# Two dense layers on one core: attention cut into more steps, put in another order among the projections, and queued behind them

## The chip, the cores and the metric

The kernel runs on one core of a Trainium2 chip. The metric is the time of one execution on the device in microseconds (us), as the median of several runs. TensorE (PE in the profile) multiplies matrices, VectorE (DVE) and ScalarE (ACT) work elementwise and read TensorE's results from PSUM, GpSimd (POOL) works elementwise in SBUF, and SyncE (SP) issues the transfers of the weights.

## The reference, cut to what matters

A first block (a token mixer and a mixture of experts) produces `x`, 256 tokens of 1024 channels. The second block puts 16 meta tokens ahead of them (272 rows) and runs two dense layers. The change touches the first half of each layer:

```python
for l in range(2):
    u = rmsnorm(h, norm_mix[l])
    proj = u @ w_in[l]                      # 13 pieces: qa ka va qi ki wi qb kb vb qc kc vc gc
    # A: 8 heads; 8 index heads score every key, the best 64 keys of a query are kept, softmax over them
    # B: 4 heads of two softmaxes each, w = p0 - lam * p1, then rmsnorm
    # C: 4 heads of retention (scores times a fixed decay), rotary q and k, rmsnorm, times silu(gc)
    h = h + concatenate([a_out, b_out, c_out]) @ w_out[l]
    u = rmsnorm(h, norm_ff[l])
    h = h + square(relu(u @ w_ff1[l])) @ w_ff2[l]
return rmsnorm(h, final_norm)[:, 16:]
```

## The kernel before

**Projections.** Activations stand with channels on the 128 partitions and the 272 tokens along the free axis. Every float32 operand is split into a high and a low part of a narrower type (`split_hl`, L148: the high part is a cast on ACT, the low part a subtraction on DVE), and a product is three matmuls per 128 input channels, high by high, high by low, low by high (`mm3`, L154, the matmul at L164). One projection (`prod`, L1609) makes 128 output channels: 8 blocks of input channels, so 24 matmuls of 272 columns. In layer 1, query-like pieces leave the meta tokens out and have 256 columns. `wload` brings 256 output channels of weights per transfer (1 MB) into a ring of four on SP's queue, which serves two projections; `parts` (L175) splits them into a ring of two.

**The mixing half of a layer** is a set of Python generators, `streams`: each `next()` traces one step. `b B u q k w c C y g` are projections (`cols`), each step one `prod`, its reading from PSUM, and for `u w y` three transposes (`to_keys`, L1661), for `c C` a rotary product (`rotated`, L1855), for `g` a silu. `I` is `indexer`: eight steps with score products (L1700) and then sixteen top-k steps that are DVE work alone (L1720, L1721). `A` is `attention`, four pairs of heads; `D` is `differential`, two pairs; `R` is `retention`, two pairs. `p` and `P` (`project`) multiply the first and the second half of the concatenated heads with `w_out`, eight steps of 12 matmuls each; before the first `p` the rest of `A`, before the first `P` the rest of `D` and `R` is traced. The projections of the indexer's inputs stand ahead of all of this and do not change.

**A step of attention before.** `attention`: scores of two query tiles, in layer 0 of the 16 meta rows too (L1788, L1797), bias plus selection on POOL (L1792), softmax (`softmax`, L1737: row minimum with the bias on DVE at L1742, exponential and row sum on ACT at L1743, reciprocal L1744, multiply L1746), end of the step; then the transposes of both heads on TensorE (`transposed`, L1755, matmuls at L1760 to L1764, copies back on ACT at L1766 and L1767), the products with the values (`pv_pair`, L1770, the matmul at L1776) and the split of the result, end of the step. `differential`: per head and query tile the scores (L1839) and two softmaxes that are joined at L1846, then two ends of a step in a row; after the tiles of a head its transposes; after both heads the value products and `head_norm` (L1806), which belong to the next step. `retention`: scores (L1881) times decay (L1883), value products and `head_norm` in one step.

**What sets the order.** `ORDER` (L1525) is a string per layer, written out by hand: one letter, one step. The order of tracing is a priority, not the issue order: the framework's scheduler fills each engine's queue from the instructions that its own reckoning has ready, the earliest traced first. So a step of attention can land in the middle of the 24 matmuls of a projection. On the chip each engine works through its queue in order. PSUM: three banks (`qm`) for results of projections and value products, two pairs (`qp`) for scores, transposes and norms, one bank (`qt`).

Of the kernel before, what the change touches and what calls it, by code (L numbers as in the profile page):

```python
# [9 lines left out]
F32 = mybir.dt.float32  # L10
F32R = mybir.dt.float32r
I32 = mybir.dt.int32
AF = mybir.ActivationFunctionType
# [140 lines left out]
def mm3(nc, out, terms, start, stop):  # L154

    n = 0
    for low in range(2):
        for wh, wl, xh, xl, fixed in terms:  # L160
            for w, x in (((wl, xh),) if low else ((wh, xh), (wh, xl))):
                l, r = (w, x) if fixed else (x, w)
                n += 1
                nc.tensor.matmul(out, l, r, start=start and n == 1, stop=stop and n == 3 * len(terms))  # L164


def load_w(k, src):
# [1280 lines left out]
def phase2_setup(k, one, tmp, psum):  # L1448
# [62 lines left out]
    for l in range(2):  # L1511
# [10 lines left out]

ORDER = ["IbIbIBIIIIIDIuDIIIqIDqIIDqkqDIIIDkIkIDwIDDDuBIIDDDDIIwDIwDIDIIIDIADDIgDgDIDDDDDAAcIkwAcDAADCCDDDAADyADyAApRpDDDRRppRpPpppPPPPPPPI",  # L1525
         "IIbIbBIIIIIDIuBIIuIDIDIDIIqqIkIDDIkIDDDIkkDIDDDIqqIDDIIIIIIAcIIwIDIDADDIDwcADDDDDDDwgDwADCACAAAyAyDADDDgARpDDDppRRpPppppPPRPPPDPP"]
T2 = 272
KT = ((0, 16), (16, 128), (144, 128))

# [1 line left out]
def phase2(k, q, A, B, out):  # L1531
# [5 lines left out]
    col = lambda name, i: vecT[:, r0[name] + i:r0[name] + i + 1]  # L1537
# [16 lines left out]
    def lgps(cols=512):  # L1554
        return pair(cols)[:, 0, :]
# [47 lines left out]
    def wload(src):  # L1603
# [2 lines left out]
        nc.sync.dma_start(w, src.rearrange("(k p) c -> p k c", p=128))  # L1606
        return w

    def prod(w, uh, ul, c0, o=None, first=True, last=True):  # L1609

        wh, wl = parts(k, w)
        m = w.shape[-1]
        if o is None:
            o = mmps(T2 - c0)
        mm3(nc, o[:m], [(wh[:, kk, :], wl[:, kk, :], uh[:, kk, c0:], ul[:, kk, c0:], True) for kk in range(w.shape[1])],
            first, last)
        return o[:m]

    nc.vector.tensor_copy(hT[:, :, 0:16], q["meT"])
# [16 lines left out]
    def layer(l, norm, end):  # L1636

        last = l == 1
# [98 lines left out]
        def softmax(pd, b, scaled, into=None):  # L1737

            m, n = pd.shape
            p = soft(m, n, "pd") if into is None else into  # L1740
            st = wk.tile([128, 3], F32, name=k.nm("st3"), tag="st3", bufs=4)[:m]
            nc.vector.tensor_tensor_reduce(p, pd, b, -1.0, 3.0e38, ALU.add, ALU.min, st[:, 0:1])  # L1742
            nc.scalar.activation(p, p, AF.Exp, bias=st[:, 0:1], scale=-1.0, accum_out=st[:, 1:2])  # L1743
            nc.vector.reciprocal(st[:, 2:3], st[:, 1:2])  # L1744
            if scaled:
                nc.vector.tensor_scalar_mul(p, p, st[:, 2:3])  # L1746
            return p, st[:, 2:3]

        def keys(t, j, n=128):
# [29 lines left out]
        def attention(hp):  # L1779

            rows = [slice(64 * i, 64 * i + 64) for i in range(2)]
            br = [bias_rows(2 * hp + i) for i in range(2)]
            p01, pm = ([], []), [None, None]
            for qt in range(2):
                ke = 144 + 128 * qt
                pd = pair(ke)
                for i in range(2):
                    nc.tensor.matmul(pd[:, i], qa[hp][rows[i], 16 + 128 * qt:144 + 128 * qt], ka[hp][rows[i], :ke],  # L1788
                                     start=True, stop=True)
                for i in range(2):  # L1790
                    bs = soft(128, ke)
                    nc.gpsimd.tensor_add(bs, bias_tile(br[i], qt), sels[qt])  # L1792
                    p01[i].append(softmax(pd[:, i], bs, True, bs)[0])
            if not last:
                pd = pair(16)
                for i in range(2):
                    nc.tensor.matmul(pd[:16, i], qa[hp][rows[i], 0:16], ka[hp][rows[i], 0:16], start=True, stop=True)  # L1797
                for i in range(2):
                    pm[i] = softmax(pd[:16, i], bmeta[:, 2 * hp + i, :], True, soft(16, 16))[0]
            yield 1  # L1800
            ts = [transposed(p01[i], pm[i], "pT") for i in range(2)]
            o = pv_pair(va[hp], ts)
            split_hl(k, cat_h[:, hp, c0:], cat_l[:, hp, c0:], o[:, c0:])
            yield 1

        def head_norm(o, gcol, extra, mul, j):  # L1806

            sq = wk.tile([128, T2], F32, name=k.nm("sq"), tag="sq", bufs=2)
            nc.scalar.activation(sq[:, c0:], o[:, c0:], AF.Square)
            pss = lgps(T2)  # L1810
            nc.tensor.matmul(pss[:, c0:], blk64, sq[:, c0:], start=True, stop=True)
            v = wk.tile([128, T2], F32, name=k.nm("nv"), tag="nv", bufs=1)
            nc.scalar.activation(v[:, c0:], pss[:, c0:], AF.Identity, scale=1.0 / 64, bias=k.eps)
            rs = wk.tile([128, T2], F32, name=k.nm("hrs"), tag="hrs", bufs=1)
            rsqrt_small(k, wk, rs[:, c0:], v[:, c0:], T2 - c0, tag="rq", full=T2)
            of = wk.tile([128, T2], F32, name=k.nm("of"), tag="of", bufs=2)
            nc.vector.scalar_tensor_tensor(of[:, c0:], o[:, c0:], gcol, rs[:, c0:], op0=ALU.mult, op1=ALU.mult)
            if mul is not None:
                nc.vector.tensor_mul(of[:, c0:], of[:, c0:], mul[:, c0:])
            if extra is not None:  # L1820
                nc.vector.tensor_scalar_mul(of[:, c0:], of[:, c0:], extra)
            split_hl(k, cat_h[:, j, c0:], cat_l[:, j, c0:], of[:, c0:])

        def differential(hp):
            ts = []
            for i in range(2):
                h = 2 * hp + i
                p01 = []
                br = bias_rows(8 + h)
                for qt in list(range(2)) + ([] if last else [2]):  # L1830
                    ke = 16 if qt == 2 else 144 + 128 * qt
                    qs = slice(0, 16) if qt == 2 else slice(16 + 128 * qt, 144 + 128 * qt)
                    nq = 16 if qt == 2 else 128
                    b = bmeta[:, 8 + h, :] if qt == 2 else bias_tile(br, qt)
                    pc, rc = [], []
                    pd = pair(ke)[:nq]
                    for c in range(2):
                        rows = slice(64 * i + 32 * c, 64 * i + 32 * c + 32)
                        nc.tensor.matmul(pd[:, c], qb[hp][rows, qs], kb[hp][rows, :ke], start=True, stop=True)  # L1839
                    for c in range(2):  # L1840
                        p, rr = softmax(pd[:, c], b, False)
                        pc.append(p)
                        rc.append(rr)
                    nc.vector.tensor_scalar(pc[1], pc[1], rc[1], nlam[:nq, l:l + 1], op0=ALU.mult, op1=ALU.mult)
                    w2 = wk.tile([128, T2], F32, name=k.nm("w2"), tag="w2", bufs=3)[:nq, :ke]
                    nc.vector.scalar_tensor_tensor(w2, pc[0], rc[0], pc[1], op0=ALU.mult, op1=ALU.add)  # L1846
                    p01.append(w2)
                    yield 1
                    yield 1
                ts.append(transposed(p01, None if last else p01[2], "pTd"))  # L1850
                yield 1
            o = pv_pair(vb[hp], ts)
            head_norm(o, col(("diff", l), 0), 1.0 - linit[l], None, 4 + hp)

        def rotated(t, cc):  # L1855
            pr = lgps(T2)
# [14 lines left out]
        def retention(hp):  # L1871
            dec, ts = [], []
            for i in range(2):
                dec.append(wk.tile([128, 656], F32, name=k.nm("dec"), tag="dec", bufs=2))
                nc.scalar.dma_start(dec[i], a["dec"][:, 2 * hp + i, :])
                ts.append(wk.tile([128, 656], F32, name=k.nm("pT"), tag="pT", bufs=2))
            for f, n, q0, d0, d1 in ((0, 16, c0, c0, 272), (16, 128, 16, 272, 528), (144, 128, 144, 528, 656)):
                pd = pair(T2)[:n, :, q0:]
                for i in range(2):
                    rows = slice(64 * i, 64 * i + 64)  # L1880
                    nc.tensor.matmul(pd[:, i], kc[hp][rows, f:f + n], qc[hp][rows, q0:], start=True, stop=True)  # L1881
                for i in range(2):
                    nc.vector.tensor_mul(ts[i][:n, d0:d1], pd[:, i], dec[i][:n, d0:d1])  # L1883
            o = pv_pair(vc[hp], ts)
            head_norm(o, col(("ret", l), hp), None, gcs[hp], 6 + hp)
            yield 1
            yield 1


# [40 lines left out]
        for c in ORDER[l]:  # L1930
            if c in "pP":
                for x in "A" if c == "p" else "DR":
                    for _ in streams[x]:
                        pass
            next(streams[c], None)
        norm, = norm
        norm.add(7)

# [114 lines left out]
```

## Time and profile before

| | |
|---|---|
| median of 3 runs | 2543.44 us (2540.8 to 2544.05) |
| the profiled execution | 2548.04 us, its span 2546.3 us |
| TensorE busy | 2323.5 us, 91% of the span |
| VectorE, ScalarE busy | 1254.0 us (49%), 918.0 us (36%) |
| mixing half of layer 0, of layer 1 | 1757 to 1968 us, 2160 to 2353 us of the span |
| their feed-forward halves | 1968 to 2143 us, 2353 to 2537 us |

A line of stretches gives the busy time of each engine and the clock that was granted to TensorE as a share of 2.4 GHz; 0.50 is its other level, 1.2 GHz. A line of waits reads: TensorE's instruction at that line waited for the engine and line behind the arrow. In a timeline the first number is the start, the second how long the run of like instructions lasted; matmuls overlap, so the price of a piece is read from start to start. A float32 matmul of the attention parts is recorded as two instructions.

### The profile page before, as it was taken

To read this page: it belongs to the slowest core of one execution; us is meant where nothing else is said; L and a number is where in the kernel's file an instruction comes from. 1 tells how busy PE (TensorE), PEld (TensorE's weight loads), DVE (VectorE), ACT (ScalarE), POOL (GpSimd) and SP (SyncE) were. 2 spreads that over 40 slices of the span, in tenths; PEclk is the share of its full clock that TensorE was granted. 3 is DMA by queue.
4 is the path that set the end of the run, shared out by engine and by line. 5 is a ranking of instruction groups with operands and counts; after the bars stand their busy time and mean duration, and the time that the engine had idled before them with its cause. 6 is when DMAs were issued, how large, how long until landed. Compare 5 with 4: busy or idle time off the path is not lost.

```text
span 2546.3 us, 36312 instructions
## 1 busy us (share of the span) xinstructions
PE 2323.5 (91%) x14402; PEld 1535.4 (60%) x14403; DVE 1254.0 (49%) x2716; ACT 918.0 (36%) x1916; POOL 148.9 (6%) x186
## 2 busy tenths in 40 slices
PE   6699878999989999999899999988989999998998
PEld 3476557889873333333333333325867999877998
DVE  4988886677551111121211111125756656766665
ACT  4556545567430101010101010113544545454544
POOL 0122122000010000000000000000010001011000
PEclk9889978999989999999999999999979999999999
DMA  8522330234979999999899999994324555523563
GB/s 280 138 81 59 128 97 26 64 87 132 301 293 379 404 415 403 416 404 397 347 416 412 416 398 415 392 403 138 111 77 143 171 177 154 156 86 121 183 185 113
DMA packets 290348, 605.88 MB, mean 238 GB/s; under 512 B 26038, under 2 KB 218681, under 8 KB 254332
## 3 DMA queue, kind: packets, MB, share of 16 engines
q1 hardware_dynamic: 283236, 595.24, 64.0%
q10 hardware_dynamic: 6280, 7.80, 1.1%
q8 instruction: 115, 1.88, 0.3%
q0 software_dynamic: 656, 0.46, 0.1%
q14 instruction: 61, 0.50, 0.1%
HBM read 602.30 MB, written 1.15 MB: 237 GB/s over the span
## 4 chain that ended last, share of the span: by engine, by line
PE 38%; DVE 5%; issue 4%; ACT 2%; POOL 1%; DMA 1%; ACTq 0%; DVEq 0%; POOLq 0%
PE qm L164 18%; PE yd L1373 5%; PE gt L1353 4%; PE lt L1353 4%; PE qm L1776 2%; PE tr L1280 1%; DVE wl L151 1%; PE tr L1336 1%; PE gt L1357 0%; PE tr L1263 0%; ACT wh L150 0%; DVE act L1256 0%; DVE g L1250 0%; DVE u L1584 0%; ACT sg L1253 0%
## 5 line engine op out<-in xcount | busy, mean ns | idle before, releaser
L150 ACT CAST wh<-w 128x1024 fp32r<-128x1024 f32 (+2 forms) x318 | 318.5, 1002 | 296.4 <-PE qm L164 210.6
L151 DVE TENSOR_TENSOR wl<-w,wh 128x1024 fp32r<-128x1024 f32 (+2 forms) x318 | 371.5, 1169 | 41.0 <-ACT wh L150 38.5
L164 PE MATMUL qm<-uh,wh 128*128 128x272 f32 (+2 forms) x1008 | 265.9, 297 | 0.5 <-ACT wh L150 0.4
L164 PE MATMUL qm<-ul,wh 128*128 128x272 f32 (+2 forms) x1008 | 263.5, 294 | 1.3 <-DVE ul L151 1.3
L1373 PE MATMUL yd<-w,aT 128*64 128x512 f32 x1024 | 259.8, 639 | 0.7 <-ACT aT L1264 0.4
L1250 DVE TENSOR_SCALAR g<-gt 128x1024 f32<-128x1024 f32 x16 | 19.6, 1225 | 409.4 <-PE gt L1357 353.9
L1252 ACT ACTIVATE sg<-g 128x1024 f32<-128x1024 f32 x16 | 16.9, 1057 | 538.5 <-DVE g L1250 538.5
L164 PEld LDWEIGHTS qm<-uh,wh 128*128 128x128 f32 (+1 forms) x1008 | 193.7, 193 | 9.4 <-issue 6.4
L164 PEld LDWEIGHTS qm<-ul,wh 128*128 128x128 f32 (+1 forms) x1008 | 194.2, 193 | 4.3 <-DVE ul L151 1.9
L1353 PE MATMUL gt<-w,resB 128*64 128x512 f32 x512 | 184.0, 598 | 0.0
L1353 PE MATMUL lt<-w,resB 128*64 128x512 f32 x512 | 181.3, 593 | 0.6 <-DVE act L1251 0.6
L1353 PE MATMUL gt<-w,xg 128*64 128x512 f32 x512 | 178.3, 595 | 0.0
L1353 PE MATMUL lt<-w,xg 128*64 128x512 f32 x512 | 177.5, 593 | 0.0
L1373 PEld LDWEIGHTS yd<-w,aT 128*64 128x64 f32 x1024 | 78.8, 148 | 162.1 <-issue 154.4
L164 PE MATMUL qm<-uh,wl 128*128 128x272 f32 (+2 forms) x1008 | 145.0, 286 | 0.0
L164 PE MATMUL mm<-hTh,wh 128*128 128x256 f32 (+1 forms) x384 | 131.6, 362 | 9.4 <-ACT wh L150 4.1
L164 PEld LDWEIGHTS qm<-uh,wl 128*128 128x128 f32 (+1 forms) x1008 | 132.5, 188 | 0.0
L164 PE MATMUL qm<-fl,wh 128*128 128x272 f32 (+1 forms) x512 | 128.5, 286 | 0.0
L164 PE MATMUL qm<-fh,wh 128*128 128x272 f32 (+1 forms) x512 | 127.3, 286 | 0.0
L164 PE MATMUL mm<-hTl,wh 128*128 128x256 f32 (+1 forms) x384 | 126.9, 350 | 0.0
L1353 PEld LDWEIGHTS lt<-w,resB 128*64 128x64 f32 x512 | 53.6, 137 | 73.0 <-issue 71.2
L164 PEld LDWEIGHTS qm<-fl,wh 128*128 128x128 f32 x512 | 96.5, 189 | 0.5
(586 smaller groups left out, 4291.4 us busy)
## 6 DMA issues: line engine op xcount, KB each, us to landing
w<-in_w_gu_dram SPq DMA_DIRECT2D x256, 1024.0 KB
w<-in_w_down_dram SPq DMA_DIRECT2D x128, 1024.0 KB
w<-in_w_ff_dram SPq DMA_DIRECT2D x64, 1024.0 KB
w<-in_w_in_dram SPq DMA_DIRECT2D x72, 512.0 KB
w<-in_w_in_dram SPq DMA_DIRECT2D x30, 1024.0 KB
y<-in_w_mod_dram SPq DMA_DIRECT2D x19, 1024.0 KB
w<-in_w_out_dram SPq DMA_DIRECT2D x24, 512.0 KB
w<-in_w_mod_dram SPq DMA_DIRECT2D x5, 1024.0 KB
```

Source lines behind the costliest of these rows:

```text
L150: k.nc.scalar.copy(hi, x)
L151: k.nc.vector.tensor_sub(lo, x, hi.bitcast(F32))
L164: nc.tensor.matmul(out, l, r, start=start and n == 1, stop=stop and n == 3 * len(terms))
L1250: nc.vector.tensor_scalar(g, gt, 7.0, LOW / 1.702, op0=ALU.min, op1=ALU.max)
L1252: nc.scalar.activation(sg, g, AF.Exp, scale=-1.702)
L1280: nc.tensor.matmul(o, spT[:, t * 128:(t + 1) * 128], ys[:, js], start=True, stop=True)
L1336: nc.tensor.matmul(o, hx[:, t, f * 128:(f + 1) * 128], S[t].rearrange("p e s -> p (e s)"), start=(t == 0 and i == 0), stop=(t == 1 and i = ...
L1353: nc.tensor.matmul(quarter(j)[64 * i:64 * i + 64], xg[:, kk, c0:c0 + CAP], w[i][:, j * 512:(j + 1) * 512], start=(kk == 0), stop=False)
L1373: nc.tensor.matmul(yd[64 * i:64 * i + 64, j * 512:(j + 1) * 512], aT[:, 2 * f2 + f, 64 * i:64 * i + 64], w[i][:, f, j * 512:(j + 1) * 512] ...
L1776: nc.tensor.matmul(o[r, f:], v[:n, j, r], keys(ts[i], j, n)[:, f - KQ[j]:], start=(j == 0), stop=(j == 2))
```

## The change

`ORDER` is a new string per layer: the same projections, each followed by a few steps of `I`, `D`, `A` or `R`. Steps are cut elsewhere: `attention` ends one behind its transposes too, `differential` loses the doubled end and gains one between the square and the norm (`squared` is split off from `head_norm`) and one at its end, `retention` ends a step behind its scores and one behind the square. `mm3` returns its last matmul, `prod` notes it, and each step of `I`, `D`, `A` or `R` is traced inside `tc.issue_after` of that matmul: what the step puts on TensorE is queued behind it, as an order of issue alone, with no wait for its end. The multiply of `softmax` goes from DVE to ACT. `retention` takes its score tiles from the tag of `differential`.

```diff
--- before.py
+++ after.py
@@ -161,7 +161,8 @@
             for w, x in (((wl, xh),) if low else ((wh, xh), (wh, xl))):
                 l, r = (w, x) if fixed else (x, w)
                 n += 1
-                nc.tensor.matmul(out, l, r, start=start and n == 1, stop=stop and n == 3 * len(terms))
+                mm = nc.tensor.matmul(out, l, r, start=start and n == 1, stop=stop and n == 3 * len(terms))
+    return mm
 
 
 def load_w(k, src):
@@ -1522,8 +1523,10 @@
 
 
 
-ORDER = ["IbIbIBIIIIIDIuDIIIqIDqIIDqkqDIIIDkIkIDwIDDDuBIIDDDDIIwDIwDIDIIIDIADDIgDgDIDDDDDAAcIkwAcDAADCCDDDAADyADyAApRpDDDRRppRpPpppPPPPPPPI",
-         "IIbIbBIIIIIDIuBIIuIDIDIDIIqqIkIDDIkIDDDIkkDIDDDIqqIDDIIIIIIAcIIwIDIDADDIDwcADDDDDDDwgDwADCACAAAyAyDADDDgARpDDDppRRpPppppPPRPPPDPP"]
+ORDER = [("bII BII bII BII uDII uDII qDII qIII qDII qDI kDII kDII kI kAD wD wAD wAAD wD cAD cAAD CD CAD yAAD yD gAD gADR "
+          "p pR p pRR p p pR p pR p p P P P P P P P P").replace(" ", ""),
+         ("bII BII bII BII uDII uDII qIII qDII qDII qDII kII kDI kID kAD wD wAD wAA wD cAD cAAD C CAD yAA yD gAD gAR "
+          "p pR p pRR p p pR p pR p p P P P P P P P P").replace(" ", "")]
 T2 = 272
 KT = ((0, 16), (16, 128), (144, 128))
 
@@ -1606,14 +1609,16 @@
         nc.sync.dma_start(w, src.rearrange("(k p) c -> p k c", p=128))
         return w
 
+    made_by = [None]
+
     def prod(w, uh, ul, c0, o=None, first=True, last=True):
 
         wh, wl = parts(k, w)
         m = w.shape[-1]
         if o is None:
             o = mmps(T2 - c0)
-        mm3(nc, o[:m], [(wh[:, kk, :], wl[:, kk, :], uh[:, kk, c0:], ul[:, kk, c0:], True) for kk in range(w.shape[1])],
-            first, last)
+        made_by[0] = mm3(nc, o[:m], [(wh[:, kk, :], wl[:, kk, :], uh[:, kk, c0:], ul[:, kk, c0:], True)
+                                     for kk in range(w.shape[1])], first, last)
         return o[:m]
 
     nc.vector.tensor_copy(hT[:, :, 0:16], q["meT"])
@@ -1743,7 +1748,7 @@
             nc.scalar.activation(p, p, AF.Exp, bias=st[:, 0:1], scale=-1.0, accum_out=st[:, 1:2])
             nc.vector.reciprocal(st[:, 2:3], st[:, 1:2])
             if scaled:
-                nc.vector.tensor_scalar_mul(p, p, st[:, 2:3])
+                nc.scalar.activation(p, p, AF.Copy, scale=st[:, 2:3])
             return p, st[:, 2:3]
 
         def keys(t, j, n=128):
@@ -1799,14 +1804,18 @@
                     pm[i] = softmax(pd[:16, i], bmeta[:, 2 * hp + i, :], True, soft(16, 16))[0]
             yield 1
             ts = [transposed(p01[i], pm[i], "pT") for i in range(2)]
+            yield 1
             o = pv_pair(va[hp], ts)
             split_hl(k, cat_h[:, hp, c0:], cat_l[:, hp, c0:], o[:, c0:])
             yield 1
 
-        def head_norm(o, gcol, extra, mul, j):
-
+        def squared(o):
             sq = wk.tile([128, T2], F32, name=k.nm("sq"), tag="sq", bufs=2)
             nc.scalar.activation(sq[:, c0:], o[:, c0:], AF.Square)
+            return sq
+
+        def head_norm(o, sq, gcol, extra, mul, j):
+
             pss = lgps(T2)
             nc.tensor.matmul(pss[:, c0:], blk64, sq[:, c0:], start=True, stop=True)
             v = wk.tile([128, T2], F32, name=k.nm("nv"), tag="nv", bufs=1)
@@ -1846,11 +1855,13 @@
                     nc.vector.scalar_tensor_tensor(w2, pc[0], rc[0], pc[1], op0=ALU.mult, op1=ALU.add)
                     p01.append(w2)
                     yield 1
-                    yield 1
                 ts.append(transposed(p01, None if last else p01[2], "pTd"))
                 yield 1
             o = pv_pair(vb[hp], ts)
-            head_norm(o, col(("diff", l), 0), 1.0 - linit[l], None, 4 + hp)
+            sq = squared(o)
+            yield 1
+            head_norm(o, sq, col(("diff", l), 0), 1.0 - linit[l], None, 4 + hp)
+            yield 1
 
         def rotated(t, cc):
             pr = lgps(T2)
@@ -1873,7 +1884,7 @@
             for i in range(2):
                 dec.append(wk.tile([128, 656], F32, name=k.nm("dec"), tag="dec", bufs=2))
                 nc.scalar.dma_start(dec[i], a["dec"][:, 2 * hp + i, :])
-                ts.append(wk.tile([128, 656], F32, name=k.nm("pT"), tag="pT", bufs=2))
+                ts.append(wk.tile([128, 656], F32, name=k.nm("pT"), tag="pTd", bufs=2))
             for f, n, q0, d0, d1 in ((0, 16, c0, c0, 272), (16, 128, 16, 272, 528), (144, 128, 144, 528, 656)):
                 pd = pair(T2)[:n, :, q0:]
                 for i in range(2):
@@ -1881,9 +1892,11 @@
                     nc.tensor.matmul(pd[:, i], kc[hp][rows, f:f + n], qc[hp][rows, q0:], start=True, stop=True)
                 for i in range(2):
                     nc.vector.tensor_mul(ts[i][:n, d0:d1], pd[:, i], dec[i][:n, d0:d1])
+            yield 1
             o = pv_pair(vc[hp], ts)
-            head_norm(o, col(("ret", l), hp), None, gcs[hp], 6 + hp)
+            sq = squared(o)
             yield 1
+            head_norm(o, sq, col(("ret", l), hp), None, gcs[hp], 6 + hp)
             yield 1
 
 
@@ -1932,7 +1945,11 @@
                 for x in "A" if c == "p" else "DR":
                     for _ in streams[x]:
                         pass
-            next(streams[c], None)
+            if c in "IDAR":
+                with tc.issue_after(made_by[0].ins):
+                    next(streams[c], None)
+            else:
+                next(streams[c], None)
         norm, = norm
         norm.add(7)
```

## Rows read from the trace of the kernel before

**Rows 1.** The page's head.

```profile
span 2546.3 us, 36312 instructions
```

**Rows 2.** Stretches: from:to and length, busy us (x instructions) by engine, clock, DMA share, GB/s.

```profile
1757.00:1968.00 211.00, 195.84 (x1298) 159.00 (x1298) 138.42 (x428) 99.94 (x246) 18.91 (x25) 0.90 0.38 113
2160.00:2353.00 193.00, 178.82 (x1267) 148.72 (x1266) 134.17 (x368) 95.31 (x216) 20.43 (x25) 0.96 0.40 120
1968.00:2143.00 175.00, 175.00 (x1391) 174.62 (x1390) 104.35 (x156) 90.09 (x128) 0.00 (x0) 1.00 0.57 177
2353.00:2537.00 184.00, 183.93 (x1550) 183.53 (x1548) 114.83 (x170) 97.23 (x143) 6.33 (x6) 1.00 0.52 164
1757.00:1840.00 83.00, 79.89 (x586) 70.72 (x586) 59.31 (x171) 38.10 (x79) 4.52 (x7) 0.98 0.45 133
1840.00:1948.00 108.00, 98.00 (x583) 71.33 (x581) 60.18 (x220) 48.90 (x141) 8.28 (x12) 0.83 0.25 73
```

**Rows 3.** The same for the projections' matmuls (L164) alone, mixing halves.

```profile
1757.00:1968.00 211.00, 135.45 (x928) 124.64 (x928) 0.90 0.38 113
2160.00:2353.00 193.00, 130.84 (x943) 120.90 (x942) 0.96 0.40 120
```

**Rows 4.** TensorE's waits, layer 0's mixing half: us in total, times, longest.

```profile
PE qp L1760 <- DVE st L1742: 3.7, 2, 2.7
PE qp L1764 <- DVE w L1846: 2.6, 2, 1.5
PE qp L1760 <- DVE pp L1746: 1.5, 2, 1.2
...
PE qp L1700 <- ACT rl L1702: 0.7, 1, 0.7
```

**Rows 5.** TensorE's waits, layer 1's mixing half.

```profile
PE qm L1776 <- ACT pT L1766: 3.7, 4, 2.4
...
PE qp L1760 <- DVE st L1742: 1.1, 1, 1.1
```

**Rows 6.** Stretches of 5 us in layer 0, columns as in group 2.

```profile
1890.00:1895.00 5.00, 5.00 (x19) 2.22 (x18) 0.44 (x1) 1.78 (x5) 1.12 (x2) 0.50 0.20 56
1895.00:1900.00 5.00, 5.00 (x22) 3.98 (x22) 0.00 (x0) 1.55 (x4) 0.00 (x0) 0.50 0.00 0
```

**Rows 7.** TensorE's timeline, one head's transposes and a pair's value products: start us, us.

```profile
1876.54 0.27 PE L1760 MATMUL qp<-cst,pp 128*16 128x128 f32 x1
...
1877.29 0.67 PE L1776 MATMUL qm<-pT,va 16*64 16x272 f32 x2
...
1879.60 0.39 PE L164 MATMUL qm<-ul,wh 128*128 128x272 f32 x1
```

**Rows 8.** TensorE's timeline, scores of two query tiles amid a projection.

```profile
2283.46 0.52 PE L1788 MATMUL qp<-ka,resA 64*128 64x144 f32 x4
2283.90 0.40 PE L164 MATMUL qm<-ul,wh 128*128 128x272 f32 x1
...
2284.73 0.73 PE L1788 MATMUL qp<-ka,resA 64*128 64x272 f32 x4
2285.39 0.39 PE L164 MATMUL qm<-uh,wh 128*128 128x272 f32 x1
```

**Rows 9.** Instructions by shape, layer 0's mixing half: busy us, mean ns, idle before.

```profile
L151 DVE TENSOR_TENSOR wl<-w,wh 128x1024 fp32r<-128x1024 f32 x30 | 37.0, 1233 | 3.8 <-ACT wh L150 3.7
...
L1743 ACT ACTIVATE pp<-pp,st 128x272 f32<-128x272 f32 x16 | 8.3, 516 | 4.8 <-DVE st L1742 4.7
...
L1746 DVE TENSOR_SCALAR pp<-pp,st 128x272 f32<-128x272 f32 x8 | 3.1, 386 | 0.1
```

**Rows 10.** The same with shapes taken together.

```profile
L1720 DVE MAX8 top<-wkr 128x8 f32<-128x144 f32 (+1 forms) x14 | 4.7, 365 | 0.0
...
L1846 DVE SCALAR_TENSOR_TENSOR w<-pp,st,pp 128x144 f32<-128x144 f32 (+1 forms) x8 | 3.7, 458 | 0.0
...
L127 ACT ACTIVATE rsy<-rsy 128x272 f32<-128x272 f32 x5 | 2.1, 427 | 0.1
```

## The prediction

> **What bounds the kernel now.** I read the page's head first, then the table of stretches for each dense layer, then TensorE's waits, and last the timeline of TensorE's instructions for the price of single pieces. The execution spans 2546.3 us [rows 1]; its own time is 2548.0 us, 4.6 above the median of the three runs, 2543.4. I make the sum as a difference and take it off the median. The diff touches only the mixing half of the two dense layers, 211 us of layer 0 and 193 us of layer 1. There TensorE is busy 195.84 and 178.82 us, VectorE (DVE) 138.42 and 134.17, ScalarE (ACT) 99.94 and 95.31 [rows 2]. So TensorE is the bound, and what can be gained is the part of its time that is not full-speed work.
>
> **That part.** In the feed-forward halves, where projections run undisturbed, a matmul of 272 columns takes 175.00/1391 = 0.126 us and one of 256 columns 183.93/1550 = 0.119 us [rows 2]. The mixing halves hold 928 and 943 such projection matmuls [rows 3]. In layer 0 that is 928 x 0.126 = 117 us. In layer 1, 528 of them have 256 columns: 528 x 0.119 + 415 x 0.126 = 115 us.
> The attention pieces I price from start to start in the timeline. The transposes of one head take 0.75 us, the twelve products with the values 2.3 less one foreign matmul, so 2.0 [rows 7]. Scores of one query tile take 0.45 and 0.66 [rows 8], the 16 meta rows some 0.15. A pair of heads of `attention` is then 1.26 + 1.5 + 2.0 = 4.8, of `differential` 2 x (1.26 + 0.75) + 2.25 = 6.3, of `retention` some 4.3 (12 score products like those of the values, 2.0 again, a norm of 0.25). Four, two and two of them with 9 us for the indexer, rotations and value transposes make 49 us in layer 0; 46 in layer 1, which has no meta queries. Floors: 117 + 49 = 166 and 115 + 46 = 161 us. **Lost today: 211 - 166 = 45 and 193 - 161 = 32, together 77 us.** No reordering can return more.
>
> Where the 77 lie:
> - Clock. The granted clock is 0.90 and 0.96 over the two halves [rows 2]: 0.10 x 211 = 21 us and 0.04 x 193 = 8 us lost. In layer 0 nearly all of it is at 1840 to 1948 us (0.83). At 1890 to 1900 us the grant is 0.50, the lower level of 1.2 GHz, with TensorE counted busy throughout but on 19 and 22 instructions in 5 us [rows 6]: small products of attention in a row, no projection among them.
> - Idle. 211 - 195.84 = 15 us and 193 - 178.82 = 14 us. In layer 0 the transposes wait for a softmax (3.7, 2.6 and 1.5 us), and the burst of eight indexer steps for its relu (0.7) [rows 4]. In layer 1 the value products wait for the copies just before them (3.7) and the transposes for a softmax (1.1) [rows 5].
> - The rest, 9 and 10 us: steps that land inside a projection. Between the two score pieces at 2283.46 and 2284.73 stand five projection matmuls that take 0.83 us instead of 0.63 [rows 8]; some 50 such places a layer at 0.2 make 10.
>
> **The change part by part.**
> *Shorter steps* (`attention`, `differential`, `retention`): a step now ends behind the transposes and behind the square, so that the copy (ACT) and the norm's input are made under the next projection, 24 x 0.126 = 3.0 us. The wait that this covers is the 3.7 of [rows 5]; no instruction is added. The value products' sum now stays in one of the three `qm` banks over one projection; two are left, and reading a result takes about 0.39 us of each 3.0, so that costs nothing. Without that room a projection would start late by those 0.39. `retention` takes its two `pT` tiles from `differential`'s tag; both `differential` pairs are through when it starts, so no wait for a buffer.
> *New order.* Before, all four `attention` pairs, one `differential` and both `retention` pairs are crowded in the 108 us from 1840; now at most three steps stand between two projections. The longest cluster (values, scores, a `differential` step, `w3 V S D`) is 2.0 + 1.26 + 0.45 = 3.7 us, then comes a projection of 3.0. The 10 us of small work that the low clock of [rows 6] sat in no longer stand together. The weights stay in their streams' order on SP's queue and each tile is used up by two neighbouring projections; the bias loads on ACT's queue move with their steps, as far ahead of their use as before. POOL's additions move along too.
> *The tie* (`issue_after`): TensorE instructions of I, D, A and R come behind the last matmul of the projection in front. It adds no semaphore, only order. Behind a tied step that is late stand all later projections, as in any in-order queue. The trace of before does not show a tied step, so bounds: all 10 us of breaks per layer back, or none (a break is only moved); I take half, since a step whose softmax is late will still land inside the next projection.
> *The multiply onto ACT* (`softmax`): per layer 16 large ones leave DVE (0.386 us for 272 columns) for ACT, where an instruction of that shape took 0.516 [rows 9]. ACT goes from 100 to some 110 us of a stretch of 190: free, under TensorE. If that cover were gone, 32 x (0.516 - 0.386) = 4 us come on the path. The Trainium skill (ScalarE: Activation LUTs, Rules for kernel authors) says that multiplications belong on VectorE, not on ScalarE; by it this edit costs those 4 us and the forecast would be 2523. The rows agree on the single price, but not on the engine that is short.
>
> **Sum.** (a) Clock: I take 8 of 21 us and 5 of 8 as left, since a cluster of 3.7 us with one wait in it may still lower the grant: -13 and -3. Bounds: all 29 back, or none. (b) Softmax and copy waits, 3.7 + 2.6 + 1.5 = 7.8 and 3.7 + 1.1 = 4.8, two thirds gone, and the indexer's 0.7 wholly, as its steps now stand two to a projection: -6 and -4. Bounds: all, or none. (c) Breaks: -5 and -5. (d) New: DVE from the first `u` to the last `k`. Per projection it has 1.23 for the low half of the weights and about 0.39 to read the result [rows 9], two top-k steps of two passes of 0.37, and a `differential` softmax of four passes near 0.46 [rows 10]: 1.6 + 1.5 + 1.8 = 4.9 us against TensorE's 3.0 + 0.6. Over seven such projections that is 9 us; the split weights are double-buffered, which hides one projection's 3, and layer 1 has no meta step: +6 and +2. Bounds: 0 (the top-k slides back, nobody waits for it before the first `attention`) and 9 + 9. (e) New: the last `retention` norm now stands right before the second half of `project`, whose every product needs it. Chain: four ACT and four DVE instructions of about 0.43 [rows 10] and the split, 4.3 us; cover is three projections' first six matmuls, 18 x 0.126 = 2.3. So +2 and +2; bounds 0 and 4 each.
> Together -16 - 10 - 10 + 8 + 4 = **-24 us: 2519 us.**
>
> **The rivals.**
> *Everything fits* (chance 0.10): (a) to (c) return nearly all of the 77 and (d), (e) cost 4 each: about -60, 2483 us. For it: DVE and ACT have room on average [rows 2]. Against: several engines near 70% in an in-order chain seldom leave none idle.
> *The gaps only move* (0.14): a softmax takes the same DVE and ACT time wherever it starts, so TensorE waits at the tied step instead, and the grant falls as before; only the breaks go, and (d), (e) eat that: -12 to +5, about 2540 us. Also what results if the tie does not do what it says, because the scheduler had the steps there already. Against: the steps stand amid projections now [rows 8].
> *Slower: VectorE's queue in front of the projections* (0.20). In order, DVE finishes top-k and softmax first and makes the next low half late; then every projection from `u` to `k` starts late. Price: 4.9 - 3.6 = 1.3 us x 9 x 2 = 23 in place of the 8 of (d), and the holes bring the lower grant there: a quarter of that stretch's 32 us of TensorE work at half speed, 8 us a layer. -24 - 8 + 23 + 16 = +7, and up to +30 if the lower grant lasts into the `attention` part: 2550 to 2573, centre 2556. It decides if DVE is over 95% busy for 20 us and TensorE's longest wait is for `wl`. For it: 59.31 of the first 83 us, 71%, already [rows 2]; against: `wl` does not stand among the long waits of [rows 4, 5].
>
> **How the numbers follow.** The forecast has the chance that its rivals leave. Forecast 0.56. About 5 us, 0.2%, is what a measurement of this kernel can tell from no change. Faster: 0.56 + 0.10 + 0.06 of the moved gaps = 0.72; same: 0.08; slower: 0.20. The forecast's own range is 2493 to 2531. For 8 in 10 I add part of both sides: from 2484 (most of the case where everything fits) to 2556 (the centre of the slower one).
>
> **What would show it.** Right: the mixing halves at about 196 and 184 us; the granted clock at 0.95 or more in both; the 1840-like stretch without a run of half clock over 7 us; the waits of transposes and value products under 4 us a layer; projection matmuls in unbroken groups of 24; ACT's busy time up by some 10 us a layer, DVE's down by 7. Wrong: a large wait for `wl` or `wh` between `u` and `k`; several us of waiting for the `cath`/`catl` split at the start of the second `project`; half clock as long as before.

## The result and the profile after

The changed kernel takes 2496.98 us as the median of 4 runs (2494.59 to 2501.63), 0.9822 of the kernel before (95% interval 0.9805 to 0.9839): 46.4 us less, where 24 were forecast. It is inside the range, on the side that was forecast, and at nearly twice the gain.

The two profiled executions compare well, since each lies some 4.6 us above its median: spans of 2546.3 and 2499.9 us. Cut at the `sum` products that open and close each mixing half, the 46.4 us between them lie like this: start of the first dense layer 3.2 earlier (work in front of it that the change does not touch; over the runs below that start lies anywhere from 1746 to 1759 us), layer 0's mixing half 28.0 shorter (209.6 to 181.6), layer 1's 13.9 shorter (191.3 to 177.4), the feed-forward halves and the end 1.3 shorter. About 42 us belong to the change; the other 4.5 lie in parts that it does not touch.

Stretches of the kernel after, columns as in [rows 2]: both mixing halves, and 80 us of the attention part.

```profile
1754.00:1936.00 182.00, 174.07 (x1293) 147.20 (x1294) 135.84 (x404) 105.91 (x269) 18.76 (x25) 1.00 0.44 129
2130.00:2307.00 177.00, 167.99 (x1273) 145.42 (x1273) 129.61 (x349) 99.45 (x231) 21.21 (x24) 0.99 0.42 127
...
1836.00:1916.00 80.00, 79.93 (x588) 62.60 (x588) 54.84 (x186) 52.21 (x152) 7.33 (x11) 1.00 0.33 98
```

The granted clock is 1.00 and 0.99 where it was 0.90 and 0.96 [rows 2]; TensorE is busy for 79.93 of the 80 us in which `attention` runs. TensorE's waits after, layer 0 and then layer 1:

```profile
PE qm L164 <- ACT cath L150: 2.9, 1, 2.9
PE qt L1670 <- DVE vT L1660: 2.3, 2, 2.0
PE qm L164 <- DVE wl L151: 1.4, 3, 0.6
PE qp L1598 <- POOL sum L1593: 1.3, 2, 1.1
```

```profile
PE qt L1670 <- DVE vT L1660: 3.0, 2, 2.0
PE qm L164 <- ACT cath L150: 2.8, 1, 2.8
PE qm L164 <- DVE wl L151: 1.6, 3, 0.8
PE qp L1598 <- POOL sum L1593: 1.1, 1, 1.1
...
PE qp L1820 <- DVE st L1747: 0.2, 1, 0.2
```

Nothing of [rows 4] is left, nor the wait for copies of [rows 5]; of waits behind a softmax 0.2 us remain. Two new waits stand in each layer: the first `vT`, and the split of the last head norm (`cath`). At the first, VectorE runs a top-k step ahead of the reading (`vT`) that TensorE's transposes, the last line here, wait for:

```profile
1789.73 0.42 DVE L1726 MATCH_REPLACE8 wkr<-top,sc 128x272 f32<-128x272 f32 x1
1790.08 0.43 DVE L1660 TENSOR_TENSOR vT<-qm,rstd 128x272 f32<-128x272 f32 x1
...
1790.56 0.50 PE L1670 MATMUL qt<-cst,vT 128*16 128x128 f32 x3 [2.04 <-DVE vT L1660]
```

The second has a plain reason in the new strings: they hold eleven `p` where `project` has eight steps, so the last three letters do nothing, and the last norm has no product of the first project behind it. The multiply on ACT, with the forms of [rows 9]:

```profile
L1748 ACT ACTIVATE pp<-pp,st 128x272 f32<-128x272 f32 x16 | 8.2, 511 | 2.8 <-DVE st L1747 2.6
...
L1751 ACT ACTIVATE pp<-pp,st 128x272 f32<-128x272 f32 x8 | 4.2, 521 | 1.1 <-DVE st L1749 1.1
```

It takes 0.521 us, as the exponential's row had said. Of the value products, for which [rows 7] shows the pieces, four of the eight pairs of a layer now run in one go, 12 in 1.40 us from start to start; the others stand in two or three pieces:

```profile
1888.05 1.48 PE L1781 MATMUL qm<-pT,va 16*64 16x272 f32 x12
1889.45 0.39 PE L164 MATMUL qm<-uh,wh 128*128 128x272 f32 x1
```

Split by TensorE's timeline (start to start, time at half clock counted half, the profile's gaps taken out), the mixing halves change so:

| us | layer 0 before, after | layer 1 before, after |
|---|---|---|
| time lost to half clock | 18.9, 0.0 | 6.7, 1.7 |
| gaps | 15.0, 7.9 | 13.1, 9.3 |
| projections and `w_out` products | 125.1, 127.1 | 123.2, 124.8 |
| value products | 16.2, 14.1 | 16.8, 13.4 |
| the rest of attention, norms | 34.4, 32.6 | 31.6, 28.2 |
| longest stretch without a projection matmul | 14.8, 3.4 | 10.1, 4.5 |
| breaks between projection matmuls over 0.15 | 57, 58 | 55, 54 |

### The profile page after: what moved, and what is told of

It is laid out like the page before. It is cut to its first block, busy times and chain, and to the rows that moved or that the text cites. A ratio compares the mean times of both kernels' runs of the same rounds, so it can differ in the third digit from the quotient of the medians.

```text
span 2499.9 us, 36297 instructions
## 1 busy us (share of the span) xinstructions
PE 2288.2 (92%) x14402; PEld 1517.2 (61%) x14403; DVE 1252.3 (50%) x2676; ACT 929.0 (37%) x1956; POOL 151.1 (6%) x186
## 4 chain that ended last, share of the span: by engine, by line
PE 42%; DVE 4%; ACT 2%; issue 2%; POOL 0%; ACTq 0%; DVEq 0%; POOLq 0%
PE qm L164 22%; PE yd L1374 5%; PE gt L1354 4%; PE lt L1354 4%; PE tr L1281 1%; PE qm L1781 1%; DVE wl L151 1%; PE tr L1337 1%; PE gt L1358 0%; PE tr L1264 0%; DVE u L1587 0%; DVE act L1257 0%; DVE g L1251 0%; DVE ul L151 0%; ACT sg L1255 0%
## 5 line engine op out<-in xcount | busy, mean ns | idle before, releaser
L164 PE MATMUL qm<-uh,wh 128*128 128x272 f32 (+2 forms) x1008 | 260.6, 293 | 0.6 <-ACT wh L150 0.5
L164 PE MATMUL qm<-ul,wh 128*128 128x272 f32 (+2 forms) x1008 | 257.4, 289 | 1.3 <-DVE ul L151 1.3
L164 PEld LDWEIGHTS qm<-uh,wh 128*128 128x128 f32 (+1 forms) x1008 | 188.4, 187 | 10.3 <-issue 5.8
L164 PEld LDWEIGHTS qm<-ul,wh 128*128 128x128 f32 (+1 forms) x1008 | 189.1, 188 | 3.5 <-DVE ul L151 1.9
L1354 PE MATMUL lt<-w,xg 128*64 128x512 f32 x512 | 177.5, 593 | 0.0
L164 PE MATMUL qm<-uh,wl 128*128 128x272 f32 (+2 forms) x1008 | 144.7, 285 | 0.0
L164 PE MATMUL mm<-hTh,wh 128*128 128x256 f32 (+1 forms) x384 | 130.9, 360 | 9.6 <-ACT wh L150 4.1
L164 PEld LDWEIGHTS qm<-uh,wl 128*128 128x128 f32 (+1 forms) x1008 | 131.8, 187 | 0.5 <-issue 0.4
L164 PE MATMUL qm<-fl,wh 128*128 128x272 f32 (+1 forms) x512 | 128.5, 286 | 0.0
L164 PE MATMUL qm<-fh,wh 128*128 128x272 f32 (+1 forms) x512 | 127.3, 286 | 0.0
L164 PE MATMUL mm<-hTl,wh 128*128 128x256 f32 (+1 forms) x384 | 126.8, 349 | 0.0
L1354 PEld LDWEIGHTS lt<-w,xg 128*64 128x64 f32 x512 | 53.4, 137 | 71.8 <-issue 71.4
```

The lines of the kernel that those rows point to most:

```text
L164: mm = nc.tensor.matmul(out, l, r, start=start and n == 1, stop=stop and n == 3 * len(terms))
L1354: nc.tensor.matmul(quarter(j)[64 * i:64 * i + 64], xg[:, kk, c0:c0 + CAP], w[i][:, j * 512:(j + 1) * 512], start=(kk == 0), stop=False)
```

## The experiments

The theory at the start was that the places of the steps in the new order do the work; rivals were the tie, the multiply on ACT and the cuts. All runs are given as ratio to the kernel before on the same chip, and by their two mixing halves in the profile, where 1 to 2 us can come from where a short stretch at half clock falls.

**The tie taken out.**

```diff
-            if c in "IDAR":
-                with tc.issue_after(made_by[0].ins):
-                    next(streams[c], None)
-            else:
-                next(streams[c], None)
+            next(streams[c], None)
```

> The changed kernel without the tie: steps and order as changed, no queueing behind the projection. If the places of the steps in the new order do the work (theory), the scheduler finds nearly the same places by itself: 2493 to 2503 us, no long stretch at half clock, the mixing halves at 183 and 178 us. If the tie does it (rival), steps slip back into projections and the half clock returns: 2515 us or more.

Measured 2502.83 us, 0.9858 (0.9837 to 0.9879), halves 183.6 and 179.2. The two kernels' TensorE queues hold the same instructions in the same order in the two layers but for one value product of `retention` in layer 1, which stands four projection matmuls earlier without the tie. The 2 us in each half go with 6.8 us at half clock in each, against 0 and 3.4. The intervals overlap and a third of a per cent lies between the medians' ratios, so a small effect is not excluded by the times; the queues give none a place. The tie does, in this order, almost nothing.

**The order of before in the new steps.** Each letter of the old strings is written as the new letters that do the same work:

```diff
-ORDER = [("bII BII bII BII uDII uDII ... kAD wD wAD wAAD wD cAD cAAD CD CAD yAAD yD gAD gADR "
+ORDER = ["IbIbIB...uBIIDDIIwDDDwDADgDgDDDAAAckwAAcDAAADDCCAAAyypRRRpRRRpppPpppPPPPPPP",
```

> The changed kernel with the order of before: each letter of the old strings stands for the same work as before, in the new steps (a step that was cut is two letters in a row); tie and multiply on ACT stay. Theory (the order does the work): back near the kernel before, 2525 to 2550 us, with 25 us or more at half clock in layer 0's mixing half and waits of the transposes for a softmax. Rival (tie or multiply on ACT do it): below 2510 us. Cut steps alone, where nothing is put between the cuts, should give nothing.

Measured 2543.13 us, 1.0013 (0.9997 to 1.003). Its halves:

```profile
1757.00:1971.00 214.00, 198.08 (x1292) 158.83 (x1291) 132.67 (x401) 105.94 (x267) 18.26 (x25) 0.89 0.37 108
2166.00:2360.00 194.00, 180.73 (x1263) 149.94 (x1263) 129.20 (x349) 100.55 (x231) 20.36 (x24) 0.95 0.38 116
```

With tie, cuts and multiply in place the old clock (0.89, 0.95), the old gaps and the old time are back. The order is what the gain needs; the three other parts without it give nothing.

**The multiply back on VectorE.**

```diff
-                nc.scalar.activation(p, p, AF.Copy, scale=st[:, 2:3])
+                nc.vector.tensor_scalar_mul(p, p, st[:, 2:3])
```

> The changed kernel with the softmax's multiply back on VectorE. If VectorE has room in the attention stretch (theory), 2494 to 2500 us, within noise of the change. If VectorE is what the order had to relieve (rival), its 7 us more per layer in the attention stretch show: waits for wl or for a softmax come back and the time is 2503 us or more. By the rule of the Trainium skill (multiplications on VectorE) it would be some 4 us faster than the change.

Measured 2503.1 us, 0.9853 (0.9827 to 0.9879), halves 181.7 and 177.0 against 181.6 and 177.4. The median is at the rival's edge, but the halves, the only place where the edit acts, are the same, and no wait for `wl` or a softmax is added. Neither engine is short there; the multiply costs nothing on either. The rule of the Trainium skill (ScalarE: Activation LUTs, Rules for kernel authors) puts it on VectorE. The price of a single one agrees (0.386 us there, 0.521 on ACT), but following the rule gains nothing here.

**Two cuts undone.**

```diff
             yield 1
-            ts = [transposed(p01[i], pm[i], "pT") for i in range(2)]
             yield 1
+            ts = [transposed(p01[i], pm[i], "pT") for i in range(2)]
             o = pv_pair(va[hp], ts)
...
-            sq = squared(o)
             yield 1
+            sq = squared(o)
             head_norm(o, sq, ...)
```

> The changed kernel with two cuts undone at unchanged places of everything else: attention's transposes stand with the value products, and the squares with the norms, so that TensorE meets copies and squares that are just being made. Theory (the cuts hide the copies): each of 8 attention pairs waits 1 to 1.5 us for copies and each of 8 norms 0.3 us for a square, 10 to 15 us: 2507 to 2512 us, and some stretches at half clock come back. Rival (the scheduler lets the next projection go first anyway): 2495 to 2500 us.

Measured 2505.61 us, 0.987 (0.9849 to 0.9891), halves 185.3 and 180.4: 3.7 and 3.0 us more than the change. The theory's sign, half its size, and not its way. The scheduler puts at most four of the next projection's 24 matmuls between the transposes of an `attention` pair and the last of its value products, and yet only 0.5 and 0.7 us of waiting for copies show. By the split of the table above, layer 0 loses 1.7 us more to half clock (behind the `cath` wait) and 1.4 more to gaps, and in both layers the value products and the other small steps take longer, 1.9 and 2.8 us, while the projections take a little less. Why the pieces take longer the runs do not show.

**The two new waits.** For the norm, the retention steps come earlier; for `vT`, the indexer's steps are also queued on VectorE behind its reading of the projection in front:

```diff
-... yD gAD gADR p pR p pRR p p pR p pR p p P P P P P P P P
+... yD gADR gADR pR pR p pR pR p p p P P P P P P P P
```

> The changed kernel with the retention steps one or two letters earlier in both orders, so that the last head norm has three products of the first project behind it. The trace of the change shows TensorE waiting 2.9 and 2.8 us for the split of that norm (cath) at the start of the second project. Theory (the wait is the norm's chain with nothing in front): both waits go, mixing halves 3 to 6 us shorter in sum, 0.9800 of before or a little under. Rival (VectorE is the bound of the tail anyway, with products, sums and the next norm): the wait turns into waits for wl and resB, mixing halves within 2 us of 181.6 and 177.4.

```diff
-            if c in "IDAR":
+            if c == "I":
+                with tc.issue_after(made_by[0].ins), tc.issue_after(read_by[0].ins):
+                    next(streams[c], None)
+            elif c in "DAR":
```

> The changed kernel where the indexer's steps are also queued on VectorE behind its reading of the projection in front. In the trace of the change TensorE waits 2.0 us in each layer for the first vT, while VectorE runs top-k steps that were traced later. Theory (the scheduler fills VectorE with top-k steps, and the reading stands behind them): the vT waits go from 2.3 and 3.0 to under 1 us, mixing halves some 2 us shorter each. Rival (VectorE has too much to do there): the wait only moves to wl or to the first attention scores, no gain.

The earlier norm: 2497.34 us, 0.9818 (0.9797 to 0.9839), halves 179.2 and 175.6; both `cath` waits are gone, 2.4 and 1.8 us of the 2.9 and 2.8 come back. The halves are as the theory had them; the times are too noisy to show it. The top-k steps: 2498.03 us, 0.9839 (0.9809 to 0.9868), halves 181.4 and 176.2; the `vT` wait goes from 2.3 to nothing and from 3.0 to 1.0, but waits for a softmax take its place (`st`, 1.1 us in layer 0), as the rival had it. Both together, with two products of the first project mixed into the second (`p p P p P P ...`):

> Earlier retention steps and the queueing of the top-k steps together, and the last two products of the first project mixed among the first of the second, so that VectorE's work per product in the tail (0.68 + 0.43 + 0.55 + 0.53 us in the second project) is spread. If all three waits are separate: vT, cath and wl waits of 7 and 7 us mostly gone, 8 to 10 us under the change, 0.978 to 0.979 of before. If VectorE bounds the tail: as the better one of the two parts alone.

```profile
1749.00:1927.00 178.00, 173.54 (x1293) 146.80 (x1292) 134.60 (x402) 105.67 (x269) 20.29 (x24) 1.00 0.43 132
2121.00:2294.00 173.00, 166.79 (x1275) 144.46 (x1276) 129.75 (x350) 99.30 (x231) 20.08 (x25) 1.00 0.43 131
```

Measured 2490.14 us, 0.9807 (0.9784 to 0.9831), halves 178.2 and 172.6: 8.2 us under the change in the profile, no half clock, and the lowest time of the study. The waits for `wl` (1.6 and 1.5) stay. The 8 us were expected, but the ratio misses the 0.978 to 0.979 expected with them, and its interval overlaps that of the change: the times alone do not separate the two.

**What of the order does it.** First, steps by twos: two projections, then the steps of both (`k w ADD w w ADAAD w c DAD ...`).

> The changed kernel with the same sequence of attention steps and the same sequence of projections, but from the first attention step on two projections stand together and then the steps of both. The TensorE time between the steps stays as it was on average. Theory (even spacing is what the new order gives: no stretch of small products long enough to lower the clock, copies under a projection): half clock comes back, 10 us or more per layer, and waits for copies (pT), 8 to 20 us in all: 2508 to 2520 us. Rival (what counts is that a softmax starts far enough ahead of its transposes): within 5 us of the change.

Measured 2499.65 us, 0.983 (0.9809 to 0.9852), halves 183.5 and 178.1. The theory falls in this form: stretches without a projection up to 6.4 us, and half clock only behind the `cath` and `vT` waits (6.8 us in each layer). So two more rivals were set against each other, the start of a softmax and longer stretches. Scores right in front of their transposes (`kD wD wAAD wAD wD cAAD cAD CD CAAD ...`):

> The changed kernel with each attention pair's scores and softmax moved right in front of its transposes, all other places as they are (scores and transposes of a pair behind the same projection, the value products behind the next). Theory (the new order gains by starting a softmax two or three projections before its transposes): TensorE meets softmaxes that have just begun, some 3 to 5 us each with half clock behind them: 10 to 20 us per layer, 2515 to 2535 us. Rival (the even places are enough, the scheduler puts the next projection in front of a late transpose): 2497 to 2503 us.

Measured 2516.78 us, 0.989 (0.9874 to 0.9907), halves 187.3 and 187.5: 5.7 and 10.1 us more. In layer 1, 13.6 us at half clock, 6.8 of them behind this wait, which the change does not have:

```profile
PE qp L1765 <- ACT pp L1751: 2.6, 4, 1.4
```

Three by three (`k w w ADD w w c AAADDD c C C AAADDD ...`), each softmax a whole group ahead:

> The changed kernel with steps crowded by threes from the first attention step on: three projections, then transposes and values of one pair, scores of the next, and three steps of differential. Softmaxes stay a whole group ahead of their transposes. If a long stretch of small products alone lowers the clock (first theory): stretches of 6 to 9 us without a projection, half clock of 10 us or more in each layer, 5 to 12 us per layer more than the change. If only late softmaxes do it (second theory): within 4 us per layer of the change, the copies' waits alone.

Measured 2519.72 us, 0.991 (0.9885 to 0.9934), halves 199.3 and 182.9: 17.7 and 5.5 us more. Layer 0's two longest stretches without a projection are 10.3 and 11.3 us, from 1857 and 1890 us:

```profile
1855.57 1.99 PE L164 MATMUL qm<-uh,wl 128*128 128x272 f32 x8 [1.97 <-DVE wl L151]
```

```profile
1855.00:1857.00 2.00, 1.43 (x7) 1.44 (x8) 2.00 (x3) 1.05 (x1) 0.00 (x0) 0.70 0.04 10
1857.00:1862.00 5.00, 4.46 (x18) 2.82 (x18) 2.97 (x5) 0.74 (x2) 2.04 (x4) 0.50 0.60 203
1862.00:1867.00 5.00, 5.00 (x20) 2.11 (x19) 0.96 (x6) 1.92 (x7) 0.64 (x1) 0.50 0.25 62
1890.00:1895.00 5.00, 3.41 (x20) 1.78 (x19) 3.66 (x17) 4.23 (x18) 0.00 (x0) 0.84 0.00 0
1895.00:1900.00 5.00, 5.00 (x21) 2.10 (x21) 0.05 (x1) 1.09 (x3) 0.00 (x0) 0.50 0.46 133
...
1902.00:1903.50 1.50, 1.50 (x7) 1.22 (x6) 0.00 (x0) 0.00 (x0) 0.00 (x0) 0.50 0.00 0
1903.60:1906.00 2.40, 2.39 (x16) 1.08 (x15) 0.97 (x3) 2.01 (x5) 0.00 (x0) 1.00 0.00 0
```

and TensorE's timeline in the second of them:

```profile
1891.39 0.28 PE L1765 MATMUL qp<-cst,pp 128*16 128x128 f32 x1 [0.92 <-DVE st L1747]
...
1892.88 0.28 PE L1765 MATMUL qp<-cst,w 128*16 128x128 f32 x1 [0.67 <-DVE w L1855]
...
1895.79 5.64 PE L1781 MATMUL qm<-pT,va 16*64 16x272 f32 x22
1901.36 0.60 PE L164 MATMUL qm<-cath,wh 128*128 128x272 f32 x1
```

Two short waits among transposes, in which the clock falls (0.84 over 1890 to 1895 us), then 22 value products at half speed, busy throughout: the picture of [rows 6]. At the other stretch the clock falls just ahead of it (0.70 over 1855 to 1857 us), as a projection's wait of 1.97 us for `wl` ends, and stays low through it, for 13.7 us. Layer 1's longest stretch is 6.4 us; its 3.4 us at half clock stand behind the `cath` wait, so the 10 us or more at half clock that the first theory wanted in each layer came in layer 0 alone. Last, the old order with the late softmaxes of two pairs in layer 0 and one in layer 1 mended (`AAAckwAAcDAAADDCCAAA` to `AAAckwAAAcDAAADDCCAA` in layer 0, where a pair had scores, transposes and values in one go):

> The kernel with the order of before (in the new steps) and one thing of it mended: where the old order had scores, transposes and value products of a pair in one go (the third and fourth pair of layer 0, the fourth of layer 1), the scores now come two projections or steps earlier or the transposes two projections later. Theory (late softmaxes make the old order slow): a good part of the 28 and 14 us comes back, mixing halves at 190 to 200 and 182 to 188 us, the stretches of 14 us without a projection gone. Rival (crowding as such): still within 5 us of 214 and 194.

Measured 2536.25 us, 0.9965 (0.9951 to 0.9979), halves 204.1 and 190.0: 10.2 and 4.1 us better than in the old order, three tenths and a quarter of the way to the change. Both miss the ranges expected, by 4 and 2 us: a stretch of 16.0 us remains in layer 0, with three waits for softmaxes in it (1.8, 1.0 and 1.8 us), and the fall in it lasts 17.1 us of the half's 30.7 at half clock. The changed kernel once more, for this group:

> The changed kernel as it is, once more, to stand beside the runs of this group: 0.980 to 0.984 of before, mixing halves within 2 us of 181.6 and 177.4 unless a short stretch at half clock falls into one.

2496.2 us, 0.9822 (0.9795 to 0.9849), halves 181.6 and 177.5.

Layer 0 in order of its longest stretch without a projection, with its time at half clock: change 3.4 and 0 us; scores late 6.0 and 3.4; by twos 6.4 and 6.8; by threes 11.3 and 27.3; kernel before 14.8 and 41.0; old order with two pairs mended 16.0 and 30.7; old order in new steps 16.0 and 47.8. The 3.4 and the 6.8 stand behind the `cath` wait and not in those stretches, so those stretches themselves cost no clock.

What the traces add is where the clock falls to 0.50. Each of the 43 falls in the mixing halves of the fourteen traces stands in or shortly behind a wait of TensorE, most of them of 0.9 to 2.9 us; in the change and in the runs near it (without the tie, multiply back, cuts undone, the two new waits, by twos) it is always the `vT` or the `cath` wait. Not every wait brings a fall: behind the same `cath` wait in layer 0 there is one in seven runs and none in the change and its repeat. In these runs the low clock lasts 3.4 or 6.8 us; in the two long stretches by threes it lasts 13.7 and 10.2, in those of the old order up to 17.1. So late softmaxes bring waits, and crowding keeps the clock low behind them and makes the stretches long; both are in the old order. Stretches with no wait in them reach 6.4 us (by threes, layer 1) and stay at 1.00; whether a longer one would lower the clock by itself no run shows. How much of the 28 us is late softmaxes and how much crowding can't be split further by these runs, as they feed each other.

## Why the prediction was right

*The bound and the account* held: TensorE, and what it lost in the two mixing halves. The floors of 166 and 161 us were too low by 8 and 5: the table above adds up to 173.8 and 166.4 after, since the projections with their breaks take 127 and 125 us, not 117 and 115.

*(a) Clock*: mis-sized. 16 us were forecast; 18.9 and 5.0 us came back, 24. The doubt that a cluster of 3.7 us with a wait in it may lower the grant did not come true: in the change the longest clusters are 3.4 and 4.5 us, only one over 3 us has a wait in it (1.0 us), and none runs at half clock; the one fall left follows the `cath` wait of layer 1. As a doubt it was sound: in the kernel before, a cluster of 4.8 us in layer 1 with a wait of 2.4 us in it had a fall.

*(b) Waits for softmax and copies*: right in kind, low in size. Two thirds were to go, and all went: 7.8 and 4.8 us of them and the indexer's 0.7. Not foreseen: the pieces themselves run shorter where fewer foreign matmuls interrupt them, value products by 2.1 and 3.4 us.

*(c) Breaks and the tie*: **the step that failed.** "All 10 us of breaks per layer back, or none ... I take half". The breaks are 57 and 55 before, 58 and 54 after: none. The step forecast an effect of the tie, and it has next to no effect, because without it the scheduler chooses the same order of the new steps; that stood as part of a rival ("the tie does not do what it says") and is true of the tie, not of the change. Projection matmuls are not in unbroken groups of 24 either.

*(d) VectorE in front of the projections*: the forecast +8 came out as the `vT` waits, 2.3 + 3.0. Its place was right, the first `u`, and so was the mechanism, top-k steps ahead of the reading. The slower rival came closer than the time tells. Of its two signs, VectorE over 95% busy for 20 us came true in both layers:

```profile
1780.00:1800.00 20.00, 17.74 (x137) 15.93 (x137) 19.86 (x72) 9.55 (x24) 0.42 (x1) 1.00 0.36 106
2159.00:2179.00 20.00, 18.02 (x142) 16.41 (x141) 19.86 (x67) 9.39 (x20) 0.91 (x2) 1.00 0.41 128
```

The other, `wl` as TensorE's longest wait, did not (1.4 and 1.6 us in a whole half, none of it in these 20 us), and behind them VectorE has room again before the last `k`. So the rival did not happen. (The 0.39 us for reading a result is the price of the softmax's multiply in [rows 9]; the reading of a projection takes 0.44, which changes nothing.)

*(e) The last norm*: forecast +2 and +2, measured 2.9 and 2.8, and removed by moving the steps. It had been named as a sign of being wrong ("several us of waiting for the `cath`/`catl` split") and as a cost in the sum; it is the second.

*The multiply*: nothing, as forecast. *The order*: forecast as the main part, and the runs show it to be the condition of all the rest.

So the sum by the measured terms is: clock 24, gaps 7.1 + 3.8 net of the new waits, shorter pieces some 2 + 5 (175.7 to 173.8, 171.6 to 166.4), together 42, and 4.5 us from outside the changed halves, which are luck: without them the time would be some 2501.5 us, still in the range. The other signs were off in size: the halves are 181.6 and 177.4 us, not 196 and 184, and between the two tables of stretches ACT is busy 6 and 4 us more, not 10, VectorE 3 and 5 less, not 7.

## What to carry to other kernels

Where small products of attention are mixed with dense projections, look in TensorE's timeline for long stretches without a dense matmul and for the waits in and ahead of them, not only for idle time in sum: here, in layer 0, 15 us of idle went with 19 us of low clock, and an order that kept the stretches to 3 or 4 us returned the clock and half of the idle time. Start a softmax two projections before its transposes, since two steps of the same pair in a row expose its whole chain, and see that every letter of a hand-written order does something: three empty `p` hid here that nothing stood behind the last norm. A tie that fixes what the scheduler does anyway costs nothing and brings nothing; compare the queues before giving it a share of the forecast.

## What had not been expected of the hardware

A fallen grant stays at 0.50 while TensorE counts as busy for 5.00 of 5 us, through 5.6 us of value products (the timeline of the steps by threes); it fell in the 5 us before, with waits in them (busy 3.41 of 5), and is back at 1.00 in the projection that starts at 1901.36 us. And the same 12 value products take 1.40 us in one go, where broken once by a projection matmul they took 2.0 [rows 7]: over a layer, 2.1 and 3.4 us for nothing but their neighbours.
